# Block transposes on VectorE and a pass through HBM in place of 208 TensorE transposes, in a hybrid delta-rule and sparse-attention layer

## The chip, the cores and the metric

The kernel runs on one core of a Trainium2 chip. Its engines work side by side, each on a queue of its own in order: TensorE (PE, with weight loads shown as PEld), VectorE (DVE), ScalarE (ACT), GpSimd (POOL) and SyncE (SP), which issues almost all DMAs here. The metric is the device time of one execution in microseconds (us), lower is better.

## The reference

One decoder layer on a sequence of 1024 tokens with 1024 channels, float32: a gated delta rule with 8 heads (in chunks), an attention in which an indexer selects 256 keys for each query, a gated merge, and a squared-ReLU MLP.

```python
h = rms_norm(x, norm_mix_g);  proj = h @ w_in
qkv = silu(causal_short_conv(g_qkv, conv_w))            # 8 heads of 128 for each of q, k, v
gq, gk, gv = l2_normalize(q) * 128**-0.5, l2_normalize(k), v
...
def step(state, xs):                                      # over the chunks of one head
    v_new = u_n - einsum('bhcd,bhde->bhce', w_n, state)
    o_n = einsum('bhcd,bhde->bhce', q_n, state) + einsum('bhij,bhje->bhie', qk_n, v_new)
    state = state * exp(gl_n)[..., None, None] + einsum('bhcd,bhce->bhde', k_n, v_new)
    return state, o_n
...
a_q = apply_partial_rope(rms_norm(a_q, q_norm_g), cos, sin)   # 8 heads of 128
a_k = apply_partial_rope(rms_norm(a_k, k_norm_g), cos, sin)   # 2 heads of 128
o_att = dsa_sparse_attention(a_q, a_k, a_v, i_q, i_k, i_w)    # top 256 of the causal keys, softmax, values
merged = sigmoid(gate_a) * o_gdn + sigmoid(gate_b) * o_att
x = x + merged @ w_out
x = x + square(relu(rms_norm(x, norm_mlp_g) @ w_mlp_up)) @ w_mlp_down
```

## The kernel before

Most products are made in three fp32r matmuls (high x high, high x low, low x high), so that their operands are split by ACT (the high part) and DVE or POOL (the low part). Tokens stand in 8 blocks of 128.

**Order.** The program's parts are Python generators, and a planner (`Weave`, its `run` and `issue` at the file's end) weaves them at build time into one fixed order for each engine. It keeps a clock that advances with PE, gives each instruction a planned duration (a 512-column fp32r matmul 0.216, a DMA `max(0.5, elements x partitions / 90000)` and `SY_LATENCY = 2.5` more until it counts as landed), and at each step lets the ready part with the lowest priority number go on. A part yields an event that it needs, such as `("keys", h)`. At run time each engine follows that order and waits by semaphores; a wait holds up everything behind it on that engine.

**Stages.** Up to 260 us the input is normalised and turned, the indexer and the attention's projections run (`dense`, `wide_dense`); `proj_post` normalises and rotates the attention's queries (four pieces) and keys (one) and writes them to HBM by tokens, as QD and KD. From then to 905 us the delta rule runs. A unit of `gdense` (one of q, k, v, z, a, b for one head; 48 matmuls of 512 columns in two halves) projects 128 channels; it has the lowest priority and so fills PE whenever nothing else is ready. Its half is drained from PSUM by ACT: into cu (`cdrain`) for k, q and v, into th (`gate`) for the gates z, a and b. `conv` makes the short convolution and the SiLU in the tiles kt, qt or t4, channels on partitions. `keys`, `queries` and `join` make each head's triangular parts (A goes through HBM in blocks of 32, ZA and ZU), and `scan` walks over its 8 blocks: p_v = um r (cc), its evacuation svn by ACT, the state update (cc, sst) and the output (oo), each waiting for the one before. `scan` needs keys and values with tokens on partitions: `decayed(h)` transposes kt on PE (the ring tt, two PSUM banks of four blocks) and ACT copies the result to kd with a scale for each token; `values(h)` does the same from t4 to vv.

From 848 us the attention is prepared (`kprep` loads KD, transposes it in 4 groups on PE, splits it in kTh and kTl). From 912 us `score` takes the 16 pairs of query block and key head in ATT's order: it loads ql, transposes its four heads on PE into a bank of the score ring ss (two banks), splits that in qh and qlo, and makes three matmuls for each head and up to 512 keys; `reduce` (DVE: add the mask, take the maximum, later scale; ACT: exp) frees the bank. `values_out` transposes the probabilities (pt), multiplies by the values (o), and `merge` gates and splits the result for `wout`, the output projection, whose matmuls (dd<-hh,m and dd<-hl,m) then have PE's lowest priority. Its split weights go to the tiles hh and hl that held the layer's input operand, so that they can be made only when the last unit of `gdense` has been multiplied. The MLP follows `wout`.

Of the kernel before, what the change touches and what calls it, by code (L numbers as in the profile page):

```python
# [9 lines left out]
F32 = mybir.dt.float32  # L10
# [10 lines left out]
P = 128  # L21
S = 1024
# [28 lines left out]
def body(tc, a, out, dbg=None):  # L51
# [44 lines left out]
    def slot(i, shape, dt):  # L96
        return w8.tile(shape, dt, name=f"w{i}")
# [51 lines left out]
    QD = dr.tile([S, H * P], F32, name="QD")  # L149
    KD = dr.tile([S, 2 * P], F32, name="KD")  # L150
# [50 lines left out]
    def after(key):  # L201
        wv.add(0, later(wv.busy["SY"] + SY_LATENCY, key))
# [474 lines left out]

    def proj_post(ready, key, nm, t, b0, nb, nh):
        yield ready
        dst = {"ak": KD, "av": VD, "aq": QD}[nm].rearrange("(b p) c -> p b c", p=P)[:, b0:b0 + nb, :]  # L680
        if nm == "aq":
            c0 = (key[0] - 3) * HALF
            dst = dst[:, :, c0:c0 + HALF]
# [24 lines left out]
        wv.done("put", *key)  # L708
        yield
        wv.done("stored", *key)  # L710


    MK = dr.tile([NB, P, S], BF16, name="MK")
# [129 lines left out]
    QS = dr.tile([H, S], F32, name="QS")  # L843
    ZA = [dr.tile([NB, 4, 32, 32], F32, name=f"ZA{h}") for h in range(H)]
    ZU = [dr.tile([NB * 4, 8, 4, 32], F32, name=f"ZU{h}") for h in range(H)]

    blk = lambda t, b: t[:, b * P:(b + 1) * P]
    st = [dict() for _ in range(H)]
# [91 lines left out]
    def conv(u):  # L940
        h, c = gunits[u]
        ct = ctile[c] + h
        yield ("gp",)
        if len(convs) > 1:
            yield ("conv", convs[-2])
        convs.append(u)
        cu = gq.tile([P, 3 + S], F32, name="cu", bufs=2)
        G_.memset(cu[:, 0:3], 0.0)
        for half in range(2):
            yield ("half", (u, half))  # L950
# [28 lines left out]
        st[h][c + "t"] = o  # L979
        if c == "q":  # L980
            yield from query_squares(h, o, cu[:, 0:S])
        wv.done("conv", u)
        wv.add(2, {"k": keys, "q": queries, "v": values}[c](h))

    def cdrain(cu, u, half):
        yield 0.2
# [127 lines left out]
    def decayed(h):  # L1114
        if h > 1:
            yield ("scan", h - 2)
        kd = gp.tile([P, NB, P], F32, name="kd", bufs=2)
        for half in range(2):
            yield tt.ready
            ps, slot_ = tt.get()  # L1120
            for i in range(4):
                PE_.transpose(ps[:, i, :], blk(st[h]["kt"], half * 4 + i), ident)
            yield
            for i in range(4):
                b = half * 4 + i
                A_.activation(kd[:, b, :], ps[:, i, :], AF.Copy, scale=egd[:, b, h:h + 1])
                if i % 2:
                    yield
            tt.free(slot_)
        st[h]["kd"] = kd  # L1130
        wv.done("decayed", h)

# [81 lines left out]


    def values(h):
        vt = st[h]["vt"]
        yield ("keys", h)
        if h > 1:
            yield ("out", h - 2)  # L1220
        av = st[h]["av"]
        vv = gp.tile([P, NB, P], F32, name="vv", bufs=2)
        for half in range(2):
            yield tt.ready
            ps, slot_ = tt.get()
            for i in range(4):
                PE_.transpose(ps[:, i, :], blk(vt, half * 4 + i), ident)
            yield
            for i in range(4):
                b = half * 4 + i  # L1230
                A_.activation(vv[:, b, :], ps[:, i, :], AF.Copy, scale=av[:, b:b + 1])
                if i % 2:
                    yield
            tt.free(slot_)
        st[h]["vv"] = vv
        wv.done("values", h)

# [115 lines left out]
    x1, lds, woh, wol = {}, {}, {}, {}  # L1353

    def kprep():
        for half in range(2):
            t = slot(1, [P, 4, 256], F32)
            SY_.dma_start(t, KD.rearrange("(b p) c -> p b c", p=P)[:, half * 4:half * 4 + 4, :])
            hs = slice(half * HALF, (half + 1) * HALF)
            yield  # L1360
            for g in range(2):
                yield tt.ready
                ps, slot_ = tt.get()
                for i in range(4):
                    PE_.transpose(ps[:, i, :], t[:, i, g * P:(g + 1) * P], ident)
                yield
                pf = ps.rearrange("p a b -> p (a b)")
                A_.activation(kTh[g][:, hs], pf, AF.Copy)
                yield
                V_.tensor_tensor(kTl[g][:, hs], pf, kTh[g][:, hs].bitcast(F32), op=OP.subtract)  # L1370
                tt.free(slot_)
        wv.done("K")
        yield from vprep(0)

# [11 lines left out]
    def loadq():  # L1386
        for idx, (qb, g) in enumerate(ATT):
            if idx > 1:
                yield ("qt", idx - 2)
            ql = pB.tile([P, 4, P], F32, name="ql", bufs=2)  # L1390
            SY_.dma_start(ql, QD[qb * P:(qb + 1) * P, g * HALF:(g + 1) * HALF].rearrange("p (h d) -> p h d", h=4))
            lds["q", idx] = ql
            if g == 0:
                if idx > 3:
# [48 lines left out]
    def score():  # L1443
        npr = 0
        for idx, (qb, g) in enumerate(ATT):
            n = (qb + 1) * P
            yield ("ql", idx)
            yield ss.ready
            ps, slot_ = ss.get()
            ps = ps.rearrange("p (a b) -> p a b", a=4)  # L1450
            for i in range(4):
# [3 lines left out]
            qh = pB.tile([P, 4, P], F32R, name="qh", bufs=2)  # L1455
            qlo = pB.tile([P, 4, P], F32R, name="qlo", bufs=2)
            A_.activation(qh, ps, AF.Copy)
            yield
            V_.tensor_tensor(qlo, ps, qh.bitcast(F32), op=OP.subtract)
            yield  # L1460
# [1008 lines left out]
```

## Time and profile before

| | |
|---|---|
| runs | 1789.18, 1789.81, 1789.82 us (median 1789.81) |
| profiled execution, its span | 1789.24 us, 1787.5 us |
| PE busy in 355 to 860 us (delta rule) | 505.0 of 505.0 us |
| DVE and ACT busy there | 382.5 and 283.7 us |
| PE busy in 912 to 941.3 us (the attention's start) | 29.0 of 29.3 us |
| PE busy in 1000 to 1100 us (attention) | 99.9 of 100 us |
| PE busy in 1600 to 1700 us (MLP) | 100 of 100 us |
| DMA: packets, share of 16 engines | 196,411; 35.3% |

Busy time is the time in which an engine has an instruction under way. Matmuls are pipelined, so two of them overlap, and one of 128 columns has a duration of 272 ns although the next can start after less; what one costs is read from the start of its successors. The granted clock was 1.00 in every stretch but the last (0.99).

### The profile page before, as it was taken

What the parts mean: (1) busy time and instruction counts of PE and PEld (TensorE: products, weight loads), DVE (VectorE), ACT (ScalarE), POOL (GpSimd) and SP (SyncE); (2) the same over time, 40 slices, a digit from 0 to 9 for tenths busy, and PEclk for the clock granted to TensorE, in tenths of its full rate; (3) what the DMA queues carried; (4) which work ended last, traced back from release to release, by engine and by line L of the source; (5) the groups of instructions that cost most, each with busy time, mean ns of one, the idle gap of its engine ahead of it and who ended that gap; (6) DMA issues with size and microseconds to landing.
All of it is one profiled execution on the core that took longest, in us unless ns stands there. A gap on an engine that the chain in (4) does not pass through costs nothing. (4 is left out here: it accounts for less than half of the span.)

```text
span 1787.5 us, 27614 instructions
## 1 busy us (share of the span) xinstructions
PE 1773.5 (99%) x9841; PEld 1486.6 (83%) x9841; DVE 1286.3 (72%) x2758; ACT 1014.8 (57%) x2074; POOL 553.1 (31%) x772
## 2 busy tenths in 40 slices
PE   9999999999999999999999999999999999999999
PEld 7987998888888888888887888888888888888887
DVE  6557658867787888975368777887666668969673
ACT  7555757656666644453447666676666664333331
POOL 0006430743362533653013211232233222222230
PEclk9999999999999999999999999999999999999999
DMA  5201242233222222332356221325454459374241
GB/s 165 84 13 48 72 130 66 51 98 73 62 75 72 54 66 57 88 85 55 101 182 201 81 92 54 105 96 171 154 169 138 148 195 372 115 253 124 95 140 49
DMA packets 196411, 198.73 MB, mean 111 GB/s; under 512 B 45145, under 2 KB 140594, under 8 KB 196274
## 3 DMA queue, kind: packets, MB, share of 16 engines
q1 hardware_dynamic: 196258, 196.98, 35.3%
q8 instruction: 77, 1.26, 0.3%
q14 instruction: 60, 0.49, 0.1%
q10 hardware_dynamic: 16, 0.00, 0.0%
HBM read 141.17 MB, written 55.77 MB: 110 GB/s over the span
## 5 line engine op out<-in xcount | busy, mean ns | idle before, releaser
L2399 PE MATMUL dd<-hh,w 128*128 128x512 f32 x1552 | 512.9, 402 | 0.0
L2399 PEld LDWEIGHTS dd<-hh,w 128*128 128x128 f32 x1552 | 285.4, 189 | 52.8 <-issue 2.1
L2399 PE MATMUL dd<-hl,w 128*128 128x512 f32 x776 | 312.1, 402 | 0.0
L2399 ACT ACTIVATE m<-m 128x512 fp32r<-128x512 f32 (+1 forms) x240 | 139.8, 625 | 78.8 <-PE o L2399 29.8
L2399 PE MATMUL dd<-hh,m 128*128 128x512 f32 x520 | 173.1, 396 | 0.1
L2399 DVE TENSOR_TENSOR m<-m,m 128x512 fp32r<-128x512 f32 (+2 forms) x184 | 141.0, 794 | 39.0 <-ACT m L2399 33.7
L2399 PEld LDWEIGHTS dd<-hl,w 128*128 128x128 f32 x776 | 146.3, 189 | 25.6 <-issue 0.4
L2399 PE MATMUL dd<-w,hh 128*128 128x256 f32 (+1 forms) x704 | 164.7, 324 | 0.0
L2399 PEld LDWEIGHTS dd<-w,hh 128*128 128x128 f32 x704 | 118.0, 190 | 9.3 <-issue 0.5
L2399 POOL TENSOR_TENSOR sx<-sx,stmp 128x60 f32<-128x60 f32 (+24 forms) x248 | 115.8, 467 | 19.4
L2399 POOL TENSOR_TENSOR stmp<-sx,um 128x60 f32<-128x60 f32 (+24 forms) x186 | 93.1, 500 | 91.6 <-DMA um<-ZA 78.0
L2399 PE MATMUL dd<-w,hl 128*128 128x256 f32 (+1 forms) x352 | 114.1, 324 | 0.0
L2399 PEld LDWEIGHTS dd<-hh,m 128*128 128x128 f32 x520 | 96.6, 188 | 18.4 <-DVE w L2399 0.7
L2399 DVE TENSOR_SCALAR_CACHE_REDUCE tkeq<-sc,cand 128x384 f16<-128x384 f32 (+3 forms) x128 | 103.3, 807 | 1.2
L2399 PE MATMUL dd<-hl,m 128*128 128x512 f32 x260 | 102.6, 395 | 0.9 <-POOL hl L2399 0.9
L2399 POOL TENSOR_TENSOR m<-m,m 128x512 f32<-128x512 f32 x48 | 69.7, 1460 | 105.6 <-DVE m L2399 58.9
L2399 ACT ACTIVATE hh<-m 128x1024 fp32r<-128x1024 f32 x44 | 45.2, 1056 | 91.2 <-PE s L2399 42.0
L2399 ACT ACTIVATE ha<-m 128x1024 fp32r<-128x1024 f32 x44 | 45.3, 1056 | 86.0 <-PE o L2399 35.1
L2399 DVE TENSOR_TENSOR w<-w,w 128x1024 fp32r<-128x1024 f32 (+1 forms) x63 | 69.2, 1100 | 24.6 <-ACT w L2399 24.4
L2399 ACT ACTIVATE tkcm<-sc,cand 128x1024 f16<-128x1024 f32 (+1 forms) x64 | 69.9, 1092 | 23.2 <-DVE cand L2399 22.2
L2399 PE MATMUL o<-hh,m 128*128 128x512 f32 x248 | 79.6, 389 | 0.0
L2399 PEld LDWEIGHTS dd<-w,hl 128*128 128x128 f32 x352 | 67.0, 190 | 4.5
(433 smaller groups left out, 4382.7 us busy)
## 6 DMA issues: line engine op xcount, KB each, us to landing
HD<-m SPq DMA_DIRECT2D x112, 256.0 KB
m<-HD SPq DMA_DIRECT2D x56, 512.0 KB
w<-in_w_in_dram SPq DMA_DIRECT2D x48, 512.0 KB
m<-in_w_mlp_up_dram SPq DMA_DIRECT2D x33, 512.0 KB
m<-in_w_mlp_down_dram SPq DMA_DIRECT2D x16, 512.0 KB
w<-in_x_dram SPq DMA_DIRECT2D x10, 512.0 KB
wraw<-in_w_in_dram SPq DMA_DIRECT2D x4, 1024.0 KB
es<-GC SPq DMA_DIRECT2D x8, 512.0 KB
```

The costliest lines, as they stand in the source:

```text
L2399: ins = f(*args, **kw)
```

## The change

Keys and values of the delta rule, and the attention's queries and keys, are no longer transposed by PE. DVE transposes within squares of 32 x 32, and DMAs put the squares in place on a way through HBM.

- `conv` for k and v starts `by_tokens`: DVE turns the finished tile in two instructions of 128 x 512 into the part of cu that is free by then; four DMAs (one for each 32 channels; pieces of 32 values, 128 B) write it to TD with tokens as rows. cu has three buffers instead of two. The tile t4 is free after DVE's turn (`("read", "v", h)`).
- `decayed` and `values` load kd and vv from TD in one DMA of 128 x 1024, and ACT scales them in place, in the same 8 instructions.
- `proj_post` turns queries and keys by DVE (4 instructions for each of the five pieces) into a new tile trn, and four DMAs write it, channels as rows, to QT (one for each key head) and KT.
- `kprep` loads KT by key head and splits it from SBUF; `score` splits ql from SBUF. The event `("qt", idx)`, which lets the load after next overwrite ql, comes after the split.

```diff
     def proj_post(ready, key, nm, t, b0, nb, nh):
...
-        SY_.dma_start(dst, t)
+        if nm == "av":
+            SY_.dma_start(VD.rearrange("(b p) c -> p b c", p=P), t)
...
+        tr = ix.tile([P, nb, nh * P], F32, name="trn")
+        for b in range(0, nb, nb // 4):
+            yield "V"
+            V_.transpose(tr[:, b:b + nb // 4], t[:, b:b + nb // 4])
+        yield
+        wv.done("stored", *key)
+        dst = (QT[key[0] - 3] if nm == "aq" else KT_).rearrange("(y i) (r j) -> r i y j", i=32, r=4)
+        for r in range(4):
+            SY_.dma_start(dst[r][:, 4 * nh * b0:4 * nh * (b0 + nb)],
+                          tr[32 * r:32 * r + 32].rearrange("p b (x j) -> p (b x) j", j=32))
         wv.done("put", *key)
...
     def conv(u):
-        if len(convs) > 1:
-            yield ("conv", convs[-2])
+        if len(convs) > 2:
+            yield ("conv", convs[-3])
...
         if c == "v" and h:
-            yield ("values", h - 1)
+            yield ("read", "v", h - 1)
...
+        if c in "kv":
+            wv.add(2, by_tokens(h, c, o, cu[:, 0:S], u))
+        else:
+            wv.done("conv", u)
...
+    def by_tokens(h, c, o, t, u):
+        for half in range(2):
+            hs = slice(half * HALF, (half + 1) * HALF)
+            yield "V"
+            V_.transpose(t[:, hs], o[:, hs])
+        yield
+        wv.done("read", c, h)
+        dst = TD[h, c].rearrange("(m i) (q j) -> q i m j", i=32, j=32)
+        for q in range(4):
+            SY_.dma_start(dst[q], t[32 * q:32 * q + 32].rearrange("p (m j) -> p m j", j=32))
+        yield
         wv.done("conv", u)
+        wv.done("turned", c, h)
...
     def decayed(h):
         if h > 1:
             yield ("scan", h - 2)
+        yield ("turned", "k", h)
         kd = gp.tile([P, NB, P], F32, name="kd", bufs=2)
-        for half in range(2):
-            yield tt.ready
-            ps, slot_ = tt.get()
-            for i in range(4):
-                PE_.transpose(ps[:, i, :], blk(st[h]["kt"], half * 4 + i), ident)
-            yield
-            for i in range(4):
-                b = half * 4 + i
-                A_.activation(kd[:, b, :], ps[:, i, :], AF.Copy, scale=egd[:, b, h:h + 1])
...
+        SY_.dma_start(kd, TD[h, "k"].rearrange("(b p) c -> p b c", p=P))
+        after(("kl", h))
+        yield ("kl", h)
+        for b in range(NB):
+            A_.activation(kd[:, b, :], kd[:, b, :], AF.Copy, scale=egd[:, b, h:h + 1])
...
     def score():
-            yield ss.ready
-            ps, slot_ = ss.get()
-            ps = ps.rearrange("p (a b) -> p a b", a=4)
-            for i in range(4):
-                PE_.transpose(ps[:, i, :], lds["q", idx][:, i, :], ident)
-            yield
-            wv.done("qt", idx)
+            ql = lds["q", idx]
...
-            A_.activation(qh, ps, AF.Copy)
+            A_.activation(qh, ql, AF.Copy)
             yield
-            V_.tensor_tensor(qlo, ps, qh.bitcast(F32), op=OP.subtract)
+            V_.tensor_tensor(qlo, ql, qh.bitcast(F32), op=OP.subtract)
             yield
-            ss.free(slot_)
+            wv.done("qt", idx)
```

`values` changes as `decayed` does, and `kprep` as `score` does.

Three places of the order show what moves. The first is PE's queue in the delta rule, in the middle of a head's scan, before the change (t is the tile of values, dd the dense filler, cc and oo the scan):

```order
L2399 MATMUL oo<-sst,qt 128x128
L2399 MATMUL dd<-hh_109,w_6413 128x512
L2399 MATMUL dd<-hh_111,w_6412 128x512
L2399 MATMUL dd<-hl_112,w_6412 128x512
L2399 MATMUL dd<-hh_111,w_6413 128x512
L2399 MATMUL dd<-hh_97,w_6590 128x512
L2399 MATMUL dd<-hl_98,w_6590 128x512
L2399 MATMUL tt<-ident,t_6600 128x128 x4
L2399 MATMUL cc<-sr,um 128x128
```

Such groups of four are gone from the new order, 52 in all (208 transposes), and no other row of PE is added or lost.

The second place is SP's and ACT's queue where one head's values go through HBM (head 4), in the new order; w is a weight load for a dense unit, svn the scan's evacuation, th the drain of a gate unit:

```order
L2405 DMA QS<-th 1x256 x4
L2405 DMA qss<-QS 128x8x1
L2405 DMA TDv_184<-cu 32x32x32 x4
L2405 DMA w_6840<-in_w_in_dram 128x8x128
L2405 DMA vv<-TDv_184 128x8x128
L2405 DMA es<-GC 128x1024
L2405 DMA w_7022<-in_w_in_dram 128x8x128
```

```order
L2405 ACTIVATE sqs<-oo,eg 128x128
L2405 ACTIVATE vv<-vv,av 128x128 x2
L2405 ACTIVATE cu<-kt 128x1024
L2405 ACTIVATE vv<-vv,av 128x128 x2
L2405 ACTIVATE svn<-cc 128x128
L2405 ACTIVATE vv<-vv,av 128x128 x4
L2405 ACTIVATE w_6954<-w_6840 128x1024
L2405 ACTIVATE th<-dd 128x512
```

SP's queue has the five DMAs between weight loads, where it had none, and in ACT's queue the scaled copies wait for a DMA with svn and th behind them.

The third place is PE's queue where the attention's scores (s) begin, before the change:

```order
L2399 MATMUL dd<-hh_103,w_10018 128x512
L2399 MATMUL s<-kTh_9715,qh 128x256
L2399 MATMUL s<-kTl_9717,qh 128x256
L2399 MATMUL s<-kTh_9715,qlo 128x256
L2399 MATMUL s<-kTh_9715,qh 128x256
L2399 MATMUL s<-kTl_9717,qh 128x256
L2399 MATMUL s<-kTh_9715,qlo 128x256
L2399 MATMUL dd<-hh_105,w_10017 128x512
L2399 MATMUL dd<-hl_106,w_10017 128x512
```

And after it:

```order
L2405 MATMUL dd<-hl_112,w_10017 128x512
L2405 MATMUL dd<-hh_111,w_10018 128x512
L2405 MATMUL s<-kTh_9835,qh 128x256
L2405 MATMUL s<-kTl_9837,qh 128x256
L2405 MATMUL s<-kTh_9835,qlo 128x256
L2405 MATMUL s<-kTh_9835,qh 128x256
L2405 MATMUL s<-kTl_9837,qh 128x256
L2405 MATMUL s<-kTh_9835,qlo 128x256
```

Before, 60 dense matmuls of the gate units stood behind the first score row; now the last of them (hh_111 is the last of the eight operand tiles) stands ahead of it, and up to the first output-projection matmul PE's queue holds only 8 short and 11 long score triples, two groups of probability transposes and two output triples.

More of the change, by code (lines that the diff above doesn't have):

```diff
@@ L148, in body @@
     gm = ix.tile([P, NB], F32, name="gm")
-    QD = dr.tile([S, H * P], F32, name="QD")
-    KD = dr.tile([S, 2 * P], F32, name="KD")
+    QT = [dr.tile([NB * 4 * P, P], F32, name=f"QT{g}") for g in range(2)]
+    KT_ = dr.tile([NB * 2 * P, P], F32, name="KT")
     GC = dr.tile([H, S], F32, name="GC")
@@ L845, in body @@
     ZU = [dr.tile([NB * 4, 8, 4, 32], F32, name=f"ZU{h}") for h in range(H)]
+    TD = {(h, c): dr.tile([S, P], F32, name=f"TD{c}{h}") for h in range(H) for c in "kv"}
     blk = lambda t, b: t[:, b * P:(b + 1) * P]
@@ L943, in conv @@
         yield ("gp",)
-        if len(convs) > 1:
-            yield ("conv", convs[-2])
+        if len(convs) > 2:
+            yield ("conv", convs[-3])
         convs.append(u)
-        cu = gq.tile([P, 3 + S], F32, name="cu", bufs=2)
+        cu = gq.tile([P, 3 + S], F32, name="cu", bufs=3)
         G_.memset(cu[:, 0:3], 0.0)
@@ L981, in conv @@
             yield from query_squares(h, o, cu[:, 0:S])
+        if c in "kv":
+            wv.add(2, by_tokens(h, c, o, cu[:, 0:S], u))
+        else:
+            wv.done("conv", u)
+        wv.add(2, {"k": keys, "q": queries, "v": values}[c](h))
+    def by_tokens(h, c, o, t, u):
[9 more added lines that the diff above has]
+        yield
         wv.done("conv", u)
-        wv.add(2, {"k": keys, "q": queries, "v": values}[c](h))
+        wv.done("turned", c, h)
     def cdrain(cu, u, half):
@@ L1216, in values @@
     def values(h):
-        vt = st[h]["vt"]
-        yield ("keys", h)
+        yield ("turned", "v", h)
         if h > 1:
             yield ("out", h - 2)
-        av = st[h]["av"]
[L1222 to L1225, printed above, removed]
-            for i in range(4):
[L1227 to L1234, printed above, removed]
+        vv = gp.tile([P, NB, P], F32, name="vv", bufs=2)
+        SY_.dma_start(vv, TD[h, "v"].rearrange("(b p) c -> p b c", p=P))
+        after(("vl", h))
+        yield ("vl", h)
+        yield ("keys", h)
+        av = st[h]["av"]
+        for b in range(NB):
+            A_.activation(vv[:, b, :], vv[:, b, :], AF.Copy, scale=av[:, b:b + 1])
+            if b % 2:
+                yield
         st[h]["vv"] = vv
@@ L1355, in kprep @@
     def kprep():
[L1356 to L1359, printed above, removed]
+        for g in range(2):
+            t = slot(1, [P, S], F32)
+            SY_.dma_start(t.rearrange("p (b t) -> p b t", t=P), KT_.rearrange("(b g d) t -> g d b t", g=2, d=P)[g])
             yield
[L1361 to L1365, printed above, removed]
+            for half in range(2):
+                hs = slice(half * HALF, (half + 1) * HALF)
+                A_.activation(kTh[g][:, hs], t[:, hs], AF.Copy)
                 yield
-                pf = ps.rearrange("p a b -> p (a b)")
-                A_.activation(kTh[g][:, hs], pf, AF.Copy)
+                V_.tensor_tensor(kTl[g][:, hs], t[:, hs], kTh[g][:, hs].bitcast(F32), op=OP.subtract)
                 yield
-                V_.tensor_tensor(kTl[g][:, hs], pf, kTh[g][:, hs].bitcast(F32), op=OP.subtract)
-                tt.free(slot_)
         wv.done("K")
@@ L1390, in loadq @@
             ql = pB.tile([P, 4, P], F32, name="ql", bufs=2)
[L1391 removed]
+            SY_.dma_start(ql, QT[g].rearrange("(b h d) t -> b d h t", h=4, d=P)[qb])
             lds["q", idx] = ql
@@ L1447, in score @@
             yield ("ql", idx)
-            yield ss.ready
-            ps, slot_ = ss.get()
-            ps = ps.rearrange("p (a b) -> p a b", a=4)
-            for i in range(4):
-                PE_.transpose(ps[:, i, :], lds["q", idx][:, i, :], ident)
+            ql = lds["q", idx]
+            qh = pB.tile([P, 4, P], F32R, name="qh", bufs=2)
+            qlo = pB.tile([P, 4, P], F32R, name="qlo", bufs=2)
+            A_.activation(qh, ql, AF.Copy)
+            yield
+            V_.tensor_tensor(qlo, ql, qh.bitcast(F32), op=OP.subtract)
             yield
             wv.done("qt", idx)
-            qh = pB.tile([P, 4, P], F32R, name="qh", bufs=2)
-            qlo = pB.tile([P, 4, P], F32R, name="qlo", bufs=2)
-            A_.activation(qh, ps, AF.Copy)
-            yield
-            V_.tensor_tensor(qlo, ps, qh.bitcast(F32), op=OP.subtract)
-            yield
-            ss.free(slot_)
             for i in range(4):
```

12 lines of the change are left out of this document (5 added, 7 removed).

## The prediction

> **What bounds the kernel now.** I read the busy times first, then TensorE's rows by stage, its waits, and the rows around the work that goes. The first row shows TensorE (PE) occupied for nearly the whole span; the second, of the view by stretches, shows the delta rule's stage, where PE is never without work while VectorE (DVE) and ScalarE (ACT) have idle time.
> ```profile
> PE 1773.5 (99%) x9841; PEld 1486.6 (83%) x9841; DVE 1286.3 (72%) x2758; ACT 1014.8 (57%) x2074; POOL 553.1 (31%) x772
> ...
> 355.00:860.00 505.00, 505.00 (x3462) 419.65 (x3461) 382.49 (x1044) 283.74 (x688) 219.49 (x474) 1.00 0.28 72
> ```
> So a matmul that goes is worth its slot on PE, as long as PE has other work to put there. A row's mean is not that slot, because matmuls overlap. These are the groups that go (208 transposes: 64 keys, 64 values, 64 queries, 16 attention keys), and PE's timeline around one group of four:
> ```profile
> L2399 PE MATMUL tt<-ident,t 128*128 128x128 f32 x64 | 9.6, 272 | 0.0
> L2399 PE MATMUL s<-ident,ql 128*128 128x128 f32 x64 | 9.6, 272 | 0.0
> L2399 PE MATMUL tt<-ident,kt 128*128 128x128 f32 x64 | 9.6, 272 | 0.0
> ...
> L2399 PE MATMUL tt<-ident,w 128*128 128x128 f32 x16 | 2.4, 272 | 0.0
> ...
> 268.72 0.39 PE L2399 MATMUL dd<-hl,w 128*128 128x512 f32 x1
> 268.95 0.39 PE L2399 MATMUL dd<-hh,w 128*128 128x512 f32 x1
> 269.18 0.60 PE L2399 MATMUL tt<-ident,kt 128*128 128x128 f32 x4
> 269.53 0.48 PE L2399 MATMUL dd<-hh,w 128*128 128x512 f32 x1
> 269.85 0.39 PE L2399 MATMUL dd<-hl,w 128*128 128x512 f32 x1
> ```
> A 512-column matmul starts every 0.23 us (268.72, 268.95, 269.18). From 269.18 to 269.85 stand four transposes and one such matmul: 0.67 - 0.23 = 0.44 us a group, 0.11 us each.
>
> **Part 1, transposes that go.** 208 / 4 = 52 groups x 0.44 = **22.9 us** off PE: 14.1 in the delta rule (32 groups), 1.8 for the attention's keys (4), 7.0 for its queries (16). By their summed busy time (9.6 + 9.6 + 9.6 + 2.4) it would be 31.2 us; I take the spacing, since busy time counts each burst's overhang. The Trainium skill ("TensorE: Matmul & The Clock Gate", Part 4) puts a transpose at about 275 ns in a kernel, which matches the 272 ns rows; 208 of those would be an estimated 57 us, and the spacing in this trace speaks against that sum.
>
> **Part 2, DVE's turns.** 32 block transposes of 128x512 for keys and values and 20 for queries and attention keys are added. The trace has only a smaller one, and a DVE operation of the new width:
> ```profile
> L2399 DVE STREAM_TRANSPOSE t<-um x18: 374/434/439, 362.2 to 849.1; 32x256 f32<-32x256 f32 x18
> ...
> L2399 DVE TENSOR_TENSOR pl<-pt,ph 128x512 fp32r<-128x512 f32 x72 | 49.2, 687 | 19.6 <-ACT ph L2399 19.2
> ```
> At 0.43 to 0.87 us (twice the smaller) I take 0.69: 52 x 0.69 = 36 us of DVE, 22 of it in the delta rule. There DVE is idle 505.0 - 382.5 = 122 us, so I charge nothing; with that cover gone the 22 us would fall on PE. ACT's scaled copies stay 128 in number, now from SBUF; a scaled copy from PSUM and a square from SBUF of the same tile bound the difference:
> ```profile
> L2399 ACT ACTIVATE vv<-tt,av 128x128 f32<-128x128 f32 x64 | 19.6, 370 | 12.8 <-PE tt L2399 12.7
> ...
> L2399 ACT ACTIVATE gj<-vv x64: 292/310/330, 379.5 to 896.1; 128x128 bf16<-128x128 f32 x64
> ```
> 370 against 310 ns: at most 0.06 us x 128 either way, 8 us of an engine that has 221 us idle in the stage. Nothing.
>
> **Part 3, the way through HBM.** Each of 16 tiles now leaves in 4 DMAs of 1024 pieces of 128 B and returns in one load of 1024 rows of 512 B, before ACT may scale it. The nearest rows are the write of A's blocks (4 DMAs of 256 pieces of 128 B, alone in the queue) and a weight load of 1024 rows of 512 B; the stretches after each give the busy share of the 16 DMA engines (next to last column).
> ```profile
> 490.87 1.78 SPq L2399 DMA_DIRECT2D ZA<-am  x4
> ...
> 509.07 0.39 SPq L2399 DMA_DIRECT2D w<-in_w_in_dram  x1
> ...
> 491.00:492.00 1.00, 1.00 0.22 32
> 492.00:493.00 1.00, 1.00 0.44 66
> 493.00:494.00 1.00, 1.00 0.21 33
> 494.00:495.00 1.00, 1.00 0.07 16
> ...
> 510.00:511.00 1.00, 1.00 (x10) 0.59 (x12) 0.96 (x2) 0.99 (x3) 0.00 (x0) 1.00 0.73 129
> 511.00:512.00 1.00, 1.00 (x13) 0.59 (x13) 1.00 (x2) 1.00 (x3) 0.30 (x2) 1.00 1.14 344
> 512.00:513.00 1.00, 1.00 (x7) 0.83 (x6) 0.65 (x4) 0.38 (x3) 0.84 (x3) 1.00 0.26 69
> ```
> 1024 pieces cost 0.22 + 0.44 + 0.21 + 0.07 = 0.94 us of all 16 engines and were through some 3.5 us after issue; 4096 cost 3.8, so 6 to 7 us. The load is through 3.4 us after issue. Together 9 to 11 us. The planner puts the consumer 8.5 of its own microseconds behind (4 x 0.5 + 2.5, then 1.5 + 2.5), and its clock runs faster than PE: 0.216 for a 512-column matmul that takes 0.23 here. So the load comes 0 to 2 us later than planned. ACT then stands still, and behind its scaled copy wait a scan evacuation (svn) and a PSUM drain (th), as ACT's rows above the prediction show; PE waits for both. Bounds: 0 to 16 x 2 = 32 us. How such waits have gone so far, POOL's and SP's for the same kind of round trip:
> ```profile
> L2399 POOL TENSOR_TENSOR stmp<-sx,um 128x60 f32<-128x60 f32 (+24 forms) x186 | 93.1, 500 | 91.6 <-DMA um<-ZA 78.0
> ...
> SPq L2399 <- DMA ZA<-am: 6.4, 5, 2.2
> ```
> POOL stands 78 us for five of them, and PE has no idle time at all in 355 to 860. ACT is closer to PE than POOL, but the row is the nearest there is, so I go near the lower end: **+2 us**. On SP, weight loads queue behind the writes and the loads; one is needed about a unit (48 matmuls, 11 us) after its issue, lands in 3.4, and so bears some 7 us of delay: nothing.
>
> **Part 4, what PE does with the freed time.** Dense matmuls of later gate units fill PE whenever the scan waits. The scan's own chain doesn't get shorter, so in the new order this filler is used up earlier. Before, 60 dense matmuls stood behind the first score row; now the last of them stands directly ahead of it. The next filler, the output projection, needs the first merged attention result, and its weights overwrite the operand tiles that the dense matmuls read. The first and last rows of that gap, the stretch, and the stretch for dense operands alone:
> ```profile
> 911.96 0.28 PE L2399 MATMUL s<-kTh,qh 128*128 128x256 f32 x1
> ...
> 945.71 0.40 PE L2399 MATMUL dd<-hh,m 128*128 128x512 f32 x1
> ...
> 912.00:941.30 29.30, 29.01 (x152) 23.98 (x151) 21.73 (x77) 18.88 (x43) 4.99 (x3) 1.00 0.60 208
> ...
> 912.00:941.30 29.30, 16.15 (x61) 10.85 (x60) 0.00 (x0) 1.68 (x2) 2.40 (x1) 1.00 0.60 208
> ...
> L2399 DVE TENSOR_SCALAR th<-th 128x512 f32<-128x512 f32 x3 | 1.3, 421 | 0.5 <-ACT th L2399 0.5
> ...
> 909.86 0.60 ACT L2399 ACTIVATE qh<-s 128x512 fp32r<-128x512 f32 x1 [0.30 <-PE s L2399]
> ...
> 910.49 0.69 DVE L2399 TENSOR_TENSOR qlo<-s,qh 128x512 fp32r<-128x512 f32 x1 [0.47 <-ACT qh L2399]
> ```
> By 941.3 PE had done 8 short score triples (24 x 0.114), 11 long ones (33 x 0.227), 2 groups of probability transposes and 2 output triples: 2.7 + 7.5 + 0.9 + 1.4 = 12.5 us. That is all that the new order holds ahead of the first output-projection matmul. DVE needs 21.7 - 1.3 = 20.4 us for the same triples (masking, maxima, scaling, splitting), and the score ring has two banks, so PE follows DVE. Ahead of it ACT's last drain (0.5), qh (0.5) and qlo (0.6) are now bare: 1.6. PE waits 20.4 + 1.6 - 12.5 = 9.5 us; with the projection's first low part (0.6) and a wait or two in the chain I take **+10.5 us**. If chain and operators meet better, 6; if the stretch keeps its old pace, 29.3 + 1.6 - 12.5 = 18.4.
>
> **Sum.** The profiled execution took 1789.24 us (span 1787.5; the median of the runs is 1789.81, 0.6 above). 1789.2 - 22.9 + 2 + 10.5 = **1779 us**.
>
> **Rivals.** *Nothing is missed*: PE's freed slots all count, because the attention's start finds other work. For it: 7.0 us of the gain lies in the attention itself. Against: the order shows no other PE row in the gap. 1789.2 - 22.9 = 1766. *The gap keeps its pace*: 18.4 instead of 10.5, 1787; for it, ACT's 18.9 us in the same chain; against it DVE's longest waits in the stretch, which were for PE's filler-laden rows and go with the filler:
> ```profile
> DVE pr L2399 <- PE s L2399: 4.7, 5, 1.8
> ```
> *The round trip is late*: for it, ACT's in-order queue and 16 loads; against it, the write of A's blocks above. It turns the sign where PE loses more than 22.9 - 10.5 + 3.6 = 16 us, 1.0 us a load; with 2 us each (upper bound) 1789.2 - 22.9 + 10.5 + 32 = 1809. The Trainium skill ("VectorE: DVE Perf Modes", The three transpose paths) warns that a plain DMA that transposes by strides is 19 times slower; the pieces here stay 128 B long after DVE's turn, and the 0.94 us above shows no such factor, so it adds no chance. *The turn isn't off PE*: excluded, the new order has exactly the 208 fewer.
>
> **Chances.** Forecast (1773 to 1785) 0.55; nothing missed (1764 to 1773) 0.15; gap at its old pace or a moderately late round trip (1785 to 1793) 0.18; late round trip beyond that 0.12. A measurement of this kernel tells 0.2%, 3.6 us, from no change: faster is below 1786.2, slower above 1793.4. Faster 0.55 + 0.15 + 0.06 = 0.76, same 0.12, slower 0.12. The range 1766 to 1792 leaves out half of the full-gain case's lower end (0.07) and the late round trip (0.13).
>
> **What would show it.** Right: the four groups gone; PE busy through the delta rule; the last dense matmul near 910 instead of 937; PE idle about 10 us within the 23 us that follow, released by DVE (pr, qlo); the first output-projection matmul near 933 instead of 945.7. Wrong: PE idle between 355 and 860 released by ACT (svn) or a DMA (kd, vv), SP waits for the turned tiles of over 3 us, DVE above 95% at 550 to 750, or the gap's rows without idle time.

## The result and the profile after

| | before | after |
|---|---|---|
| time, median of 4 runs each | 1789.65 us | 1799.93 us (1798.63 to 1800.58) |
| ratio, 95% interval | | 1.0059 (1.0047 to 1.0072) |
| profiled execution, its span | 1789.24 us, 1787.5 us | 1798.63 us, 1796.9 us |

The change made the kernel slower by 0.6%, where 1779 us were forecast. The busy times of the changed kernel's page show that the transposes are gone from PE (11.0 us less busy than before) and that PE is idle 20.4 us longer:

```profile
span 1796.9 us, 27454 instructions
## 1 busy us (share of the span) xinstructions
PE 1762.5 (98%) x9633; PEld 1470.3 (82%) x9633; DVE 1318.2 (73%) x2810; ACT 1016.6 (57%) x2074; POOL 536.8 (30%) x772
```

The view by stretches tells where. Its columns are the stretch, its length, the busy time of PE, PEld, DVE, ACT and POOL (with the number of instructions), the granted clock, the share of the DMA engines and GB/s. Before:

```profile
0.00:300.00 300.00, 292.90 (x1727) 256.83 (x1728) 196.99 (x450) 186.77 (x412) 71.14 (x99) 1.00 0.26 80
360.00:860.00 500.00, 500.00 (x3438) 415.46 (x3437) 378.66 (x1031) 279.31 (x679) 219.49 (x474) 1.00 0.28 72
900.00:950.00 50.00, 49.71 (x258) 41.03 (x256) 34.83 (x104) 28.43 (x59) 8.24 (x6) 1.00 0.62 203
1100.00:1200.00 100.00, 98.77 (x536) 82.31 (x534) 83.53 (x187) 70.04 (x144) 28.73 (x20) 1.00 0.23 74
```

After:

```profile
0.00:300.00 300.00, 290.86 (x1712) 254.60 (x1713) 212.39 (x474) 188.04 (x413) 69.81 (x99) 1.00 0.34 83
360.00:860.00 500.00, 499.57 (x3335) 413.78 (x3336) 396.85 (x1065) 281.56 (x676) 207.63 (x474) 1.00 0.40 97
900.00:950.00 50.00, 42.42 (x185) 31.82 (x185) 34.61 (x115) 28.61 (x63) 11.51 (x8) 0.86 0.65 212
1100.00:1200.00 100.00, 90.06 (x458) 73.82 (x457) 74.69 (x169) 63.51 (x131) 27.84 (x20) 0.97 0.22 72
```

The delta rule (360 to 860) is as full as before: PE is idle there for 0.4 us, and the way through HBM costs it no more than that. PE waits above all in two places: **the first gap**, at 900 to 950, where the attention begins (7.3 us more idle, clock 0.86), and **the second gap**, at 1100 to 1200, where the attention ends and the MLP begins (8.7 us more idle). PE's rows in the first gap, from the last dense matmul to the first one of the output projection:

```profile
911.96 0.39 PE L2405 MATMUL dd<-hh,w 128*128 128x512 f32 x1
913.55 0.39 PE L2405 MATMUL s<-kTh,qh 128*128 128x256 f32 x1 [1.21 <-ACT qh L2405]
...
916.97 0.58 PE L2405 MATMUL s<-kTh,qh 128*128 128x256 f32 x1 [0.84 <-DVE nm L2405]
...
922.40 0.47 PE L2405 MATMUL pt<-ident,pr 128*128 128x128 f32 x1 [2.08 <-ACT pr L2405]
...
939.84 0.39 PE L2405 MATMUL dd<-hh,m 128*128 128x512 f32 x1
```

27.9 us lie between them for the 12.5 us of work that the prediction counted: 15.4 us lost, where it took 10.5. In the second gap PE waits for DVE's scaling of the attention's last residuals (w), and the clock falls to half after it:

```profile
1163.32 0.33 PE L2405 MATMUL s<-ident,w 128*128 128x128 f32 x1 [2.68 <-DVE w L2405]
1165.33 1.08 PE L2405 MATMUL s<-ident,w 128*128 128x128 f32 x2 [1.68 <-DVE w L2405]
...
1160.00:1165.00 5.00, 0.97 (x7) 0.54 (x5) 4.78 (x7) 1.97 (x5) 2.53 (x2) 1.00 0.70 210
1165.00:1170.00 5.00, 4.55 (x16) 3.87 (x17) 3.91 (x8) 3.11 (x7) 0.00 (x0) 0.50 0.83 250
```

**A second count.** Idle time misses waits that are shorter than the overlap of two matmuls. So I also took, from PE's timeline, each matmul's distance to the next start, less the usual distance of its form in the kernel before. This "lost" time holds idle time, short waits and a halved clock alike. Numbers below that are called lost are of this count.

| lost us | 0-300 | 300-900 | 900-950 | 950-1100 | 1100-1300 | later | sum |
|---|---|---|---|---|---|---|---|
| before | 18.0 | 48.1 | 2.4 | 8.7 | 7.5 | 1.3 | 85.9 |
| after | 20.6 | 45.8 | 16.3 | 9.5 | 21.5 | 2.4 | 116.0 |

30.1 us more are lost for 22.9 us of work that went: +7.2 of the +9.4 between the two profiled executions; 2.2 stay unexplained. The count hangs on what is taken as usual: with the median of each shape the 30.1 are 28.8, so its entries are good to about 1 us.

**Why the last head is not earlier.** The last scan row stands at 901.69, against 895.32 before, though PE has 14 us less to do by then:

```profile
895.32 0.38 PE L2399 MATMUL oo<-svn,es 128*128 128x128 f32 x2
...
901.69 0.38 PE L2405 MATMUL oo<-svn,es 128*128 128x128 f32 x2
```

The head before the last did come earlier (its last scan row is at 820.7 instead of 835.3). The last head waits for its inverse, whose way through HBM stands in SP's timeline: A's blocks are written at 785.49 before and 791.42 after, and the result is read back at 840.64 and 847.67. The way itself takes about as long in both (55.2 and 56.3 us); A is late when it sets out.

```profile
785.49 1.85 SPq L2399 DMA_DIRECT2D ZA<-am  x4
840.64 2.81 SPq L2399 DMA_DIRECT2D um<-ZU  x4
...
791.42 1.80 SPq L2405 DMA_DIRECT2D ZA<-am  x4
847.67 1.92 SPq L2405 DMA_DIRECT2D um<-ZU  x4
```

A is made by DVE, whose last step on it is a scaling (am):

```profile
779.94 1.22 DVE L2399 TENSOR_TENSOR am<-am,ck 128x1024 f32<-128x1024 f32 x1
...
790.18 1.22 DVE L2405 TENSOR_TENSOR am<-am,ck 128x1024 f32<-128x1024 f32 x1
```

The keys themselves are not late in the changed kernel (their last operation starts at 754.14, before at 758.04). The delay comes behind them, in the chain of small operations (rk, rkt) that makes the scale: before, it runs from 776.35 to the scaling at 779.94; after, it starts at 776.00 and reaches the scaling at 790.18, because operations of the last masks, of the queries' convolution (qt) and of the scan stand between its steps in DVE's order. A shorter stretch shows what the prediction's 355 to 860 averaged away. In 700 to 780 DVE was busy for 93% of the time even before the change, because the attention's masks are made there beside the last head's keys:

```profile
700.00:780.00 80.00, 80.00 (x520) 66.37 (x519) 74.64 (x168) 38.75 (x94) 44.78 (x68) 1.00 0.27 74
```

DVE's new turns have the assumed size: 0.70 us each, 32 and 20 of them.

```profile
L2405 DVE STREAM_TRANSPOSE cu<-kt x16: 671/702/707, 270.5 to 758.8; 128x512 f32<-128x512 f32 x16
...
L2405 DVE STREAM_TRANSPOSE trn<-pj x16: 668/700/712, 153.0 to 256.6; 128x512 f32<-128x512 f32 x16
```

### The profile page after: what moved, and what is told of

Its sections match the earlier page's. It is cut to its first block, busy times and chain, and to the rows that moved or that the text cites. A ratio compares the mean times of both kernels' runs of the same rounds, so it can differ in the third digit from the quotient of the medians.

```text
span 1796.9 us, 27454 instructions
## 1 busy us (share of the span) xinstructions
PE 1762.5 (98%) x9633; PEld 1470.3 (82%) x9633; DVE 1318.2 (73%) x2810; ACT 1016.6 (57%) x2074; POOL 536.8 (30%) x772
## 4 chain that ended last, share of the span: by engine, by line
PE 88%; DVE 5%; ACT 2%; DMA 2%; POOL 2%; issue 1%; SPq 0%; POOLq 0%; DVEq 0%; ACTq 0%
PE dd L2405 52%; PE o L2405 15%; PE s L2405 7%; PE pt L2405 6%; PE tt L2405 2%; PE cc L2405 2%; PE oo L2405 1%; PE sq L2405 1%; DVE w L2405 1%; PE jj L2405 1%; POOL pj L2405 1%; DVE pr L2405 0%; SPq L2405 0%; POOL ras L2405 0%; DMA w<-in_x_dram 0%
## 5 line engine op out<-in xcount | busy, mean ns | idle before, releaser
L2405 POOL TENSOR_TENSOR stmp<-sx,um 128x60 f32<-128x60 f32 (+24 forms) x186 | 83.9, 451 | 108.9 <-DMA um<-ZA 76.4
L2405 POOL TENSOR_TENSOR sx<-sx,stmp 128x60 f32<-128x60 f32 (+24 forms) x248 | 106.9, 431 | 19.4
L2405 ACT ACTIVATE tkcm<-sc,cand 128x896 f16<-128x896 f32 x64 | 69.7, 1089 | 30.6 <-DVE cand L2405 28.6
L2405 ACT ACTIVATE w<-w 128x1024 fp32r<-128x1024 f32 x48 | 50.7, 1056 | 36.9 <-PE dd L2405 36.7
```

What stands on the lines that cost most here:

```text
L2405: ins = f(*args, **kw)
```

## The experiments

Four causes were open: the two gaps, the half clock after them, DVE's turns, and the way through HBM. All times are medians; before stood at 1788.9 to 1789.2 beside them.

### The two halves, the clock, and more filler

**attention_only** takes the delta rule's functions (`conv`, `decayed`, `values`) from before; **delta_only** takes the attention's (`proj_post`, `kprep`, `loadq`, `score`). **filling** and **early2** are the changed kernel with

```diff
+    def filling():
+        yield ("drained", last, 0)
+        ps = pd.tile([P, HALF], F32, name="dd")
+        while ("mm", 0) not in wv.ev:
+            PE_.matmul(ps, kTh[0][:, :P], kTh[0][:, :HALF], start=True, stop=True)
+            yield 0.0
...
     wv.add(9, wout())
+    wv.add(10, filling())
```

```diff
-EARLY = 3
+EARLY = 2
```

> Only the attention's queries and keys are turned by DVE and HBM (20 groups of transposes less on PE, 1.8 + 7.0 us); the delta rule's keys and values go through PE as before. Theory A (the place of the filler): although PE's rows of the delta rule's heads are those of before, the new order has 9 dense matmuls behind the first score row instead of 60, and 63 output-projection matmuls behind the last score row instead of 92, so both gaps of the changed kernel appear, with the clock at half after them: 1792 to 1800 us, PE idle 10 to 15 us between the last dense and the first projection matmul. Rival B (the delta rule's way through HBM costs the time): no gap at 912 to 940, clock 1.00 throughout, 1789.2 - 8.8 = 1780.4 us.

> Only the delta rule's keys and values are turned by DVE and HBM (32 groups less on PE, 14.1 us); the attention is as before. Theory A (the place of the filler): 2 dense matmuls behind the first score row, so the first gap appears (10 to 15 us of PE idle, clock at half for about 10 us), but 92 output-projection matmuls stand behind the last score row as before, so no second gap: 1789.2 - 14.1 + about 2.5 of waits + 10 of gap + 5 of clock = 1788 to 1796 us. Rival B (the way through HBM stalls the scan): PE idle in 360 to 900, time above 1800. Rival C (the delta part is a gain, only the attention's part loses): 1775 to 1780 us.

> The changed kernel with 42 matmuls of 512 columns (0.23 us each, 9.7 us) added at the lowest priority in the first gap, between the last dense and the first output-projection matmul; nobody reads their result. Theory A (PE's wait makes the clock fall, and the fall costs about as much again): the clock stays near 1.00 from 912 to 940, the score matmuls start 0.115 and 0.23 us apart instead of 0.21 and 0.43, the first projection matmul comes 2 to 5 us sooner than 939.8, and the time falls to 1795 to 1798 us. Rival B (DVE sets the pace of this stretch, the clock costs nothing there): first projection matmul at 940 or later, time 1799 to 1809 us.

> The changed kernel with one unit of the dense filler (48 matmuls, 11 us; the b gate of head 2) moved from the early list to the end of the list. 24 dense matmuls instead of none stand behind the first score row. Theory A (what is missing is filler at the attention's start): the first gap's PE idle falls from 15 us to below 10, PE still has no idle time in 360 to 860, the time falls by 5 to 9 us, to 1791 to 1795 us; the second gap stays. Rival B (the gap is set by the chain of DVE and ACT whatever filler stands there): 1799 to 1801 us, or PE idle appears in the delta rule instead.

| | time | ratio (95%) | lost 900-950 | lost 1100-1300 |
|---|---|---|---|---|
| attention_only | 1813.0 | 1.013 (1.0115 to 1.0145) | 10.3 | 23.2 |
| delta_only | 1785.0 | 0.9976 (0.9967 to 0.9985) | 11.1 | 7.5 |
| filling | 1798.9 | 1.0054 (1.0039 to 1.0069) | 8.2 | 20.3 |
| early2 | 1792.4 | 1.0019 (1.0009 to 1.0029) | 6.3 | 21.0 |

The stretches of the first two, in this order:

```profile
900.00:950.00 50.00, 45.49 (x214) 35.49 (x212) 30.60 (x102) 23.51 (x57) 8.51 (x5) 0.97 0.53 176
1100.00:1200.00 100.00, 89.16 (x456) 72.50 (x455) 73.72 (x178) 59.27 (x122) 20.80 (x16) 0.97 0.23 74
...
900.00:950.00 50.00, 44.76 (x218) 34.47 (x217) 35.40 (x108) 32.41 (x68) 15.07 (x11) 0.97 0.71 233
1100.00:1200.00 100.00, 98.78 (x533) 82.29 (x532) 83.10 (x181) 69.94 (x145) 28.07 (x20) 1.00 0.26 85
```

The delta rule's half is a small gain, and its 14.1 us are mostly eaten by the first gap (8.7 more lost). Its 1785.0 lies above C's range and below A's, so neither is right for it: the first gap is there, as A said, but smaller. The attention's half loses 24 us though PE has 8.8 us less to do; it has both gaps, as theory A said, but is 13 us above A's range, so A was not complete. The way through HBM of keys and values, B's cause there, has no part in that kernel. In filling the clock stayed at 1.00, yet the first projection matmul came at 939.79 instead of 939.84:

```profile
910.00:940.00 30.00, 26.26 (x124) 20.36 (x123) 20.98 (x77) 17.47 (x42) 7.57 (x5) 1.00 0.88 283
...
939.79 0.40 PE L2413 MATMUL dd<-hh,m 128*128 128x512 f32 x1
```

So B holds there, though it narrowly misses both its bounds (940 and 1799): DVE and ACT set the pace of the first gap, and the half clock costs nothing that the time shows. (Its lower lost time is that of the added matmuls, which fill waits.)

Not all of that pace is work. In the changed kernel ACT stands for 3 us on a load of the attention's values (w<-VD), which it turns into vh, with the exponentials of the scores (pr) behind it in its order; PE's longest wait in the gap, 2.08 us, is for pr:

```profile
914.32 1.06 ACT L2399 ACTIVATE vh<-w 128x1024 fp32r<-128x1024 f32 x1
...
921.00 1.06 ACT L2405 ACTIVATE vh<-w 128x1024 fp32r<-128x1024 f32 x1 [3.02 <-DMA w<-VD]
```

The load lands about 6 us after its issue in both kernels. But in SP's queue it stands behind the write of the last gate, and that gate is now finished directly ahead of the scores: the load is issued 1.4 us behind the first score row, where it stood 3.8 us ahead of it before. In filling ACT waits 3.06 us for it as well; in delta_only, which has the first gap too, ACT doesn't wait for it. What it is worth was not tested by itself.

More filler does help (early2, at 1792.4 within A's range).

### What the attention's half loses by

**turns_unread** is the kernel before with only the 20 turns added; **attention_no_turn** is attention_only without them (`tr = t`, so that queries and keys leave untransposed and are not those of the reference); **queries_unread** is the changed kernel with the queries' transposes back on PE; **delta_early2** is delta_only with `EARLY = 2`.

```diff
         SY_.dma_start(dst, t)
+        if nm != "av":
+            tr = ix.tile([P, nb, nh * P], F32, name="trn")
+            for b in range(0, nb, nb // 4):
+                yield "V"
+                V_.transpose(tr[:, b:b + nb // 4], t[:, b:b + nb // 4])
+            yield
```

```diff
             ql = lds["q", idx]
+            yield ss.ready
+            ps, slot_ = ss.get()
+            for i in range(4):
+                PE_.transpose(ps[:, i * P:(i + 1) * P], ql[:, i, :], ident)
+            ss.free(slot_)
+            yield
```

> The kernel before with the 20 DVE turns of the attention's queries and keys added (0.69 us each, 14 us of DVE) and nothing else changed: the turned tile is read by nobody, PE's 208 transposes and all DMAs are those of before. Theory A (the turns stand in DVE's order ahead of work that the delta rule and the dense units need, so that the last head's scan begins later in the order and the dense filler is used up ahead of it): last scan row at 903 to 910 instead of 895.3, 9 dense matmuls behind the first score row instead of 60, the first gap appears (8 to 12 us lost at 900 to 950), 3 to 4 us more lost before 300, no second gap: 1798 to 1804 us. Rival B (14 us of DVE beside PE cost nothing): 1787 to 1791 us.

> The kernel with the attention's part alone (1813.0 us), without the 20 DVE turns: the untransposed tile is written by the same DMAs, so queries and keys are not those of the reference, while PE's rows and all transfers are the same. Theory A: 53 dense matmuls stand behind the first score row, the first gap goes and the early losses go, the second gap (63 output-projection matmuls behind the last score row, 10 to 14 us lost at 1130 to 1300) stays: 1789.2 - 8.8 + 10 to 14 = 1790 to 1797 us. Rival B (the turns are hidden, the loss is in the DMAs or in the missing transposes): 1809 us or more.

> The changed kernel with the 64 transposes of the queries put back on PE at their old place in the score ring, their result read by nobody: 7.0 us more work for PE. Theory A (PE's freed slots in the attention only pull the output projection forward, so that its rows are missing at the end of the attention): 92 instead of 63 output-projection matmuls stand behind the last score row, the loss at 1130 to 1200 falls from 19 to below 9 us with the clock at 1.00, so the 7 us of added work cost nothing: 1793 to 1799 us. Rival B (PE's slots are worth their time): 1799.9 + 7.0 = 1807 us.

> The delta rule's part alone (1785.0 us) with one unit of the dense filler (48 matmuls) moved from the early list to the end. Theory A (the 14.1 us of freed slots are real once filler is left for the attention's start): 80 dense matmuls stand behind the first score row, the loss at 900 to 950 falls from 11 to about 2.5 us, PE has no idle time in 360 to 860: 1775 to 1779 us. Rival B (the filler is then missing in the delta rule, or the first gap stays): PE idle or lost time there, 1783 to 1788 us.

| | time | ratio (95%) | lost 0-300 | lost 900-950 | lost 1100-1300 |
|---|---|---|---|---|---|
| turns_unread | 1804.0 | 1.0086 (1.0071 to 1.0101) | 22.2 | 10.0 | 8.5 |
| attention_no_turn | 1798.2 | 1.0056 (1.0041 to 1.0071) | 18.2 | 3.5 | 19.7 |
| queries_unread | 1793.6 | 1.0025 (1.0014 to 1.0036) | 22.2 | 18.8 | 8.1 |
| delta_early2 | 1782.7 | 0.9965 (0.9952 to 0.9978) | 19.0 | 6.2 | 9.3 |

Twenty DVE operations that nobody reads, 14 us of an engine that has 500 us idle, cost 15 us. The last scan row moves from 895.32 to 910.50. DVE's timeline where the last head's keys are made (kt, four operations) shows them between those of the masks (tkcm, tkeq, sc), with no idle time from 754 to 760:

```profile
754.31 1.30 DVE L2405 SCALAR_TENSOR_TENSOR kt<-cu,vecs,kt 128x1024 f32<-128x1024 f32 x1
755.53 1.25 DVE L2405 SCALAR_TENSOR_TENSOR tkeq<-sc,thr,tkcm 128x896 f16<-128x896 f32 x1
...
769.42 1.34 DVE L2405 SCALAR_TENSOR_TENSOR kt<-cu,kt 128x1024 f32<-128x1024 f32 x1
```

The last of them starts at 769.42; before, it was at 758.04. Without the turns the first gap and the early loss go, and the second gap stays (1798.2, a little above A's range). And 7.0 us of useless work put *back* on PE make the changed kernel 6.3 us faster, because the second gap closes:

```profile
1100.00:1200.00 100.00, 98.74 (x525) 81.75 (x525) 82.65 (x188) 68.50 (x142) 29.16 (x20) 1.00 0.24 78
```

delta_early2 fell between the two theories (1782.7) and decides little.

### Relief for DVE, and a control

**turns_relieved** is turns_unread with three DVE operations for each mask left out, so that ties at the selection's threshold are no longer settled. **before_early2** is the kernel before with `EARLY = 2`. **delta_masks_pool** is delta_only with the masks' last operation on POOL; **delta_early2_masks_pool** has both.

```diff
-            V_.tensor_scalar(eq[:, :n], scores[qb], th, None, op0=OP.is_equal)
...
-            V_.scalar_tensor_tensor(eq[:, :n], scores[qb], th, cum[:, :n], op0=OP.is_gt, op1=OP.add)
+            V_.tensor_scalar(eq[:, :n], scores[qb], th, None, op0=OP.is_ge)
```

```diff
-            yield "V"
-            V_.tensor_scalar(masks[qb], eq[:, :n], -1.0, -NEG, op0=OP.add, op1=OP.mult)
+            yield "G"
+            G_.tensor_scalar(masks[qb], eq[:, :n], -1.0, -NEG, op0=OP.add, op1=OP.mult)
```

> The kernel before with the 20 unread DVE turns (1804.0 us), and with DVE relieved where the last head's keys are made: of the making of the attention's masks, the three operations for each of six query blocks that settle ties at the threshold are left out (21.5 us of DVE in the rows of before, 707 to 768 us). Theory A (DVE is full from 700 to 780, so that what is added to its queue delays the last head's inverse, and the filler is used up ahead of that head): A's blocks of the last head are written at 785 to 790 instead of 799.7, the last scan row is at 893 to 898 instead of 910.5, 61 instead of 9 dense matmuls stand behind the first score row: 1788 to 1793 us. Rival B (the turns cost their time where they stand, before 300 us): 1800 to 1804 us.

> The kernel before with one unit of the dense filler moved from the early list to the end: a control for the two runs that moved it in changed kernels. Theory A (more filler at the end is worth something only where the first gap is open; before loses only 2.4 us at 900 to 950): no gain, 1787 to 1797 us. Rival B (this order of the units is better by itself): 1781 to 1786 us, which would take that part of the gain of the other two runs away.

> The delta rule's part alone (1785.0 us) with the last operation of each of the six masks moved from DVE to POOL, which is idle for most of 690 to 790. Theory A (DVE's load there decides when the last head begins): last scan row at 885 to 890 instead of 895.5, 41 instead of 2 dense matmuls behind the first score row, the loss at 900 to 950 falls from 11 to about 4 us: 1776 to 1781 us. Rival B (the last head is late for another reason, or POOL's operations hold up the last inverse): 1784 us or more.

> Both relief measures together on the delta rule's part alone: one unit of filler moved to the end (1782.7 us alone) and the masks' last operation on POOL. 91 dense matmuls stand behind the first score row. Theory A: all of the 14.1 us of freed slots but the losses at 0 to 300 count: 1775 to 1780 us. Rival B (with 80 matmuls behind that row there was enough filler already, and what is lost then is DVE's pace in the attention): no more gain, 1781 to 1784 us.

| | time | ratio (95%) | last scan row | lost 300-900 | lost 900-950 |
|---|---|---|---|---|---|
| turns_relieved | 1794.4 | 1.0028 (1.0017 to 1.0039) | 898.2 | 48.9 | 2.1 |
| before_early2 | 1806.2 | 1.0095 (1.0078 to 1.0112) | 900.9 | 57.7 | 1.9 |
| delta_masks_pool | 1781.0 | 0.9957 (0.9942 to 0.9972) | 889.2 | 49.5 | 3.9 |
| delta_early2_masks_pool | 1789.0 | 0.9999 (0.9989 to 1.0008) | 882.6 | 53.8 | 2.8 |

With DVE relieved, the kernel with the 20 turns stands 5 us above before instead of 15, and the first gap is closed; the time is 1 us above A's range, and what remains lies mostly before 300 (lost 21.5). The relief was not run without the turns, so how much of the 10 us it would save in a kernel without them is not shown. The control went worse than either theory: in the kernel before, the moved unit is missing at 360 to 450, where nothing was missing in the changed kernel:

```profile
360.00:450.00 90.00, 84.54 (x625) 69.83 (x624) 62.00 (x205) 54.52 (x130) 39.32 (x107) 0.94 0.33 86
```

PE is idle there for 5.5 of the 17 us that this kernel lost; the rest was not followed. So early2's gain is not one that the kernel before could have had. delta_masks_pool, at the upper end of A's range, is the fastest kernel here that computes the whole layer: with less DVE work there, the last head comes 6 us earlier and the first gap shrinks, though the 20 early turns have no part in it. Both relief measures together missed both theories (1789.0): they only moved the loss (PE busy 105.5 of 110 us at 750 to 860).

### The changed kernel, cause by cause

The three last kernels are the changed one with the masks' relief, then also with the queries' unread transposes, then also with `EARLY = 2`, by the diffs above.

> The changed kernel (1799.9 us) with DVE relieved as in the run before: the three operations for each of six masks that settle ties at the threshold are left out. 24 dense matmuls instead of none stand behind the first score row, 63 output-projection matmuls behind the last one as before the relief. Theory A (DVE's load delays the last head, which opens the first gap; the second gap has another cause): last scan row at 888 to 896 instead of 901.7, PE's busy time in 900 to 950 rises from 42.4 to above 46 us, the second gap stays (about 90 of 100 us at 1100 to 1200): 1788 to 1794 us. Rival B (DVE's load there is not what delays the last head of the changed kernel): 1797 to 1801 us.

> The same, and the 64 transposes of the queries put back on PE with their result read by nobody (7.0 us of added PE work), so that 92 output-projection matmuls stand behind the last score row. Theory A (the two gaps are separate and add up): PE's busy time in 1100 to 1200 is above 98 us, and the time is that of the run beside it less 5 to 7 us: 1782 to 1789 us. Rival B (closing both gaps only moves PE's idle time to a third place): at or above the run beside it.

> The same, and one unit of filler moved to the end of the list: 75 dense matmuls behind the first score row (before the change: 60). Theory A (what is left of the first gap goes): PE's busy time in 900 to 950 above 48.5 us; of the 22.9 us, 7.0 are put back and 3 to 4 are lost before 300: 1789 - 15.9 + 4 = 1777, with some remainder 1776 to 1783 us. Rival B (the moved unit is missing in the delta rule, as it was in the kernel before, where this cost 17 us): PE idle in 360 to 860, 1786 us or more.

| | time | ratio (95%) | lost 900-950 | lost 1100-1300 | lost in all |
|---|---|---|---|---|---|
| after | 1799.9 | 1.0059 (1.0047 to 1.0072) | 16.3 | 21.5 | 116.0 |
| changed_relieved | 1791.1 | 1.0013 (1.0003 to 1.0022) | 6.1 | 20.0 | 106.8 |
| changed_relieved_queries | 1781.5 | 0.9958 (0.9944 to 0.9973) | 5.8 | 7.1 | 90.5 |
| changed_all_relief | 1780.8 | 0.9959 (0.9945 to 0.9974) | 6.5 | 7.4 | 89.6 |

The same stretches of the first two:

```profile
900.00:950.00 50.00, 46.96 (x229) 37.00 (x229) 38.20 (x114) 36.16 (x74) 17.45 (x12) 1.00 0.76 254
1100.00:1200.00 100.00, 89.65 (x465) 73.43 (x464) 75.86 (x158) 62.64 (x130) 25.04 (x18) 0.97 0.21 69
...
900.00:950.00 50.00, 47.16 (x241) 38.18 (x241) 35.59 (x112) 36.06 (x74) 18.16 (x13) 1.00 0.78 254
1100.00:1200.00 100.00, 98.73 (x526) 81.89 (x525) 83.99 (x177) 69.46 (x143) 26.09 (x18) 1.00 0.28 94
```

Theory A holds for the first step. The second is larger than it expected (9.5 us, not 5 to 7), and its time 0.5 us below A's range. The two gaps have separate causes: relieving DVE at the last head is worth 8.8 us (its last scan row comes at 891.2, A's scaling at 775.50), and closing the second gap 9.5 us, though 7.0 us of work are put back for it. They don't simply add up: without the relief the same transposes were worth 6.3 us, beside a first gap that grew (18.8 lost instead of 16.3). These three kernels also leave out DVE work that the kernel before does, so their ratios are not what the change would be worth without its gaps. Some 6 us are lost at 900 to 950 even with 75 dense matmuls behind the first score row (PE busy for 47.67 of 50 us, where 48.5 were expected), and the third step gained almost nothing: what is lost there then was not traced further.

## Why the prediction was wrong

**Part 1** (22.9 us off PE) was right as a count of work. It failed as a gain for the 7.0 us of the queries: a slot is worth something only while other work can follow, and the attention's only filler, the output projection, is limited by the merged results. It was used up earlier (63 instead of 92 of its matmuls stand behind the last score row) and missing at the end. That second gap, 14.0 us more lost at 1100 to 1300, is in no step of the prediction. Its rival *nothing is missed* took those 7.0 us as the argument in its favour.

**Part 2** had the duration right (0.70 against 0.69 us) and the step "so I charge nothing" wrong. The cover of 122 us was a mean over 505 us; in 700 to 780, where the last head's keys are made, DVE had 5.4 us left. The 20 early turns alone cost 15 us, shown both ways: added to the kernel before (1804.0) and taken out of the attention's half (1813.0 to 1798.2). In the changed kernel relieving DVE there gained 8.8 us (1799.9 to 1791.1); that is the worth of the relief, and the price of the delta rule's 32 turns was not measured by itself. Why turns at 153 to 257 us put the last head behind the masks 500 us later was not followed step by step; the order is fixed at build time, and only its outcome was measured.

**Part 3** (+2 us) was about right. PE is idle for 0.4 us in 360 to 860 and loses 2.3 us less than before in 300 to 900; between 355 and 900 ACT waits for the new loads but four times and twice (us in all, times, longest):

```profile
ACT kd L2405 <- DMA kd<-TDk: 7.3, 4, 3.5
ACT vv L2405 <- DMA vv<-TDv: 1.5, 2, 0.9
```

One of its signs of being wrong did come: SP waited for the turned tiles (cu) for up to 9.1 us at once, 51.9 us in all between 355 and 860. But PE's idle time there stays at 0.4 us. So the rival *the round trip is late*, the only one that was to make the kernel slower, was not what did.

**Part 4** had the mechanism right and the size too small: 15.4 instead of 10.5 us (13.9 more lost). Its step "PE follows DVE" let DVE work for 20.4 us without a break. DVE's work is as long as counted, but it fills only 20.6 of the 27.9 us: DVE too waits, longest for ACT's exponentials behind the values' load (2.50 us), a wait that the sum had at nothing. Its sentence "the scan's own chain doesn't get shorter" was too kind: with the last head's inverse late by DVE, 188 instead of 96 dense matmuls stand in PE's order between the last two heads' outputs (oo).

From 1779 to the profiled 1798.6 the terms are: second gap 14.0, first gap 3.4 more, before 300 us 2.6, later stretches 1.9, the delta rule 4.3 less, and 2.2 that no count shows. The sign was lost by the second gap and by DVE's load at the last head.

## What to carry to other kernels

On an engine that is full, freed slots are worth only what the next shortage of filler leaves of them: look for the last stretch that each kind of filler has to cover, at each change of stage, and ask whether the work pulled forward will be missing there. Before an engine's idle time is taken as cover, cut the stage into pieces around the chain that ends last, and look at the order there; a mean of 76% can hold 80 us at 93%. And put the removed work back as an unread copy: where the kernel gets faster, the slot was filler.

## What the runs showed of the hardware

The granted clock fell to half without any long wait. PE's stretches of one microsecond in the changed kernel (length, PE busy, clock, DMA share, GB/s):

```profile
912.00:913.00 1.00, 0.35 (x2) 1.00 0.30 119
913.00:914.00 1.00, 0.45 (x2) 1.00 0.00 0
914.00:915.00 1.00, 0.78 (x5) 1.00 0.72 250
915.00:916.00 1.00, 0.96 (x7) 0.89 0.87 257
916.00:917.00 1.00, 0.16 (x2) 0.50 0.99 281
...
926.00:927.00 1.00, 1.00 (x3) 0.50 0.97 377
...
929.00:930.00 1.00, 1.00 (x6) 0.78 0.99 377
930.00:931.00 1.00, 1.00 (x6) 1.00 0.99 397
```

In the four microseconds from 912 to 916, in which the clock fell (near 915.8, as 0.89 is the mean of 915 to 916), PE was busy for 2.5 of 4 us, and its longest wait was 1.21 us; the full clock came back near 929.4 (0.78 in 929 to 930), some 3.5 us after PE's last break, which ended at 925.94. The Trainium skill ("TensorE: Matmul & The Clock Gate", Part 1) gives a window of about 3.4 us for both ways, and its table ("Why this matters for your kernels") warns of idle gaps above about 3 us. The way back agrees with the trace; the fall came with shorter waits than that table names. Here the half clock cost nothing that could be seen in the first gap, as filling showed; what it cost in the second wasn't measured by itself.
